# Weight queue, transposes, last pairs, tail squares, output queues and four pads in a one-layer attention kernel

## Chip, core and metric

The kernel runs on one core of one Trainium2 chip, in one launch. The metric is the device time of an execution in microseconds (us). The profile is one execution's trace; its engines are PE (TensorE products, with PEld for their weight loads), DVE (VectorE), ACT (ScalarE), POOL (GpSimd) and SP (SyncE, which issues DMAs).

## What is computed

One decoder layer on x of 256 x 1024 floats, then a final norm:

```
xn   = rmsnorm(x) * norm_g
q,k,v,z = xn @ w_in                  # 1024 x 4096
o    = softmax(q k^T / 8 - slope * distance, causal) v     # 16 heads of 64
h    = x + (o * silu(z)) @ w_out     # 1024 x 1024
out  = rmsnorm(h) * final_g
```

With 256 tokens the block selection of the reference has one block only, so attention is plain causal softmax with a distance bias.

## The kernel before

Every large product is made of three products of rounded parts: each fp32 operand is split into a high part and the rest, and high x high, high x low and low x high are summed in one PSUM bank. So every weight tile must be loaded by DMA, cast on ACT (`split`, L243), and subtracted on DVE (L246) before PE can use it.

The stages follow each other on PE:

- **Start.** 14 products on zeros (`warm`), transposes of x (`x_transpose`, L291, four chunks c of 256 columns, 4 transposes each) and of the gain. x comes in eight DMAs of 128 KB, the value weights in rows of 512 KB (row 0 in two halves), all issued by SP.
- **V** (L313 to 328): for each of 8 rows d of the value weights, four groups of three products with 512 moving columns (the weights move; the gained x, in `gh` and `gl`, is stationary).
- **Z, then Q and K** (`cols_unit`, L272): 8 units for the gate, then 8 pairs of one q unit and one k unit. A unit is 24 products with 256 moving columns (the normed x, in `nh` and `nlo`, moves; the weights, in `wh` and `wl`, are stationary).
- **Pairs** (L443 to 485): after each pair's units, two heads' scores, softmax on DVE and ACT, transposes of the probabilities, product with v, the gate.
- **O** (L497 to 516): output rows like V, for token halves j = 0 and 1; rows 0 to 3 of w_out first, rows 4 to 7 piece by piece (`PIECES`: 512 and 512 columns for j = 0; 512, 256 and 256 for j = 1).
- **Tail** (L507 to 565): for each piece the residual is added on DVE, squares are summed, POOL takes the power -1/2, the result is scaled by it and by final_g and stored.

The order on each engine is not the order in the text. `Plan` (L30) takes every task with an engine, a cost, a due time and its reads and writes, runs a list schedule with these costs (the earliest possible start first, then the smallest due time), and the instructions are emitted in that order. Each engine then executes its own instructions in order. Due times come from constants (`ROW`, `UNIT`, `PAIR`, L176). A due time of `FIRST` (-1000) puts a task ahead of everything that is ready. `load_row` and `load_cols` rotate through five buffers `raw`, `split` through five pairs `wh`, `wl`. All tiles lie one behind the other in SBUF in the order of their `sb` lines (L129 to 152).

Of the kernel before, what the change touches and what calls it, by code (L numbers as in the profile page):

```python
# [106 lines left out]
def hybrid_trunk(ctx: ExitStack, tc: tile.TileContext, x, norm_g, w_in, w_out, final_g, out):  # L107
# [17 lines left out]
    def sb(name, shape, dtype=F32):  # L125
        return one.tile(shape, dtype, name=name)
# [25 lines left out]
    ssf, ssq, rf = sb("ssf", [P, NS, 2]), sb("ssq", [P, 1]), sb("rf", [P, NS])  # L152
    bank = [ps.tile([P, 512], F32, name=f"bank{i}") for i in range(8)]

# [21 lines left out]
    ROW, UNIT = 2.82, 2.81  # L176
    PAIR = 2 * UNIT + 2.3
# [22 lines left out]
    def load_row(key, w, t, c0, due, parts=1):  # L200

        if t % 2 == 0:
            slot[key, t] = next_raw()
        s = slot[key, t] = slot[key, t - t % 2]
        n = D // parts
        for i in range(parts):
            o = (t % 2) * D + i * n
            dma(512 / parts, due, raw[s][:, o:o + n], w[:, t, c0 + i * n:c0 + i * n + n],
                [("raw", s, t % 2, k) for k in range(2)[i if parts == 2 else 0:i + 1 if parts == 2 else 2]])
# [53 lines left out]
    def row_mm(key, t, j, b, cols, ah, al, reads, due, start, stop, first=None):  # L263

        s = spl[key, t]
        n = cols.stop - cols.start
        q = slice(j * P, (j + 1) * P)
        add(T, 0.00137 * n, due,
            lambda: mm3(bank[b][:, :n], ah[:, t, q], al[:, t, q], wh[s][:, cols], wl[s][:, cols], start, stop),
            reads + split_of(s, sorted({cols.start // 512, (cols.stop - 1) // 512})), [("b", b)])  # L270

    def cols_unit(key, u, b, due):  # L272
        s = spl[key, u]
        h_, l_ = (w[s].rearrange("p (t e) -> p t e", t=ND) for w in (wh, wl))

        def step(g):
            for d in (2 * g, 2 * g + 1):
                mm3_cols(bank[b][:, :S], h_[:, d, :], l_[:, d, :], nh[:, d, :], nlo[:, d, :], d == 0, d == ND - 1)
        for g in range(4):
            add(T, 0.70, due + 0.70 * g, lambda g=g: step(g), split_of(s) + [("n", g)], [("b", b)], lat=0.25)  # L280


    add(Q, 0.01, 0.05, lambda: nc.sync.dma_start(gr, norm_g[0].rearrange("(t p) -> t p", p=P)), [], ["gr"])
# [18 lines left out]
    load_row("v", wi, 0, 2 * D, 0.2, parts=2)  # L302
# [140 lines left out]
    for p in range(NP):  # L443
# [9 lines left out]
        E = base + 2 * UNIT + 0.3  # L453
        n, m = p % NQ, p % NN
        add(A, 0.81, base + UNIT + 0.9, lambda p=p, b=bq: hi_q(p, b), [("b", bq)], [("qh", n)])
        add(V, 0.84, base + UNIT + 1.9, lambda p=p, b=bq: lo_q(p, b), [("b", bq), ("qh", n)], [("ql", n)])
        for a in range(2):
            add(A, 0.41, E + 0.4 + 0.4 * a, lambda p=p, b=bk, a=a: hi_k(p, b, a), [("b", bk)], [("kh", n, a)])
            add(Q, 0.2, E + 0.8 + 0.4 * a, lambda p=p, a=a: dup_k(p, a), [("kh", n, a)], [("kd", n, a)])
            add(V, 0.42, E + 1.0 + 0.4 * a, lambda p=p, b=bk, a=a: lo_k(p, b, a), [("b", bk), ("kh", n, a)],  # L460
                [("kl", n, a)])
        add(T, 0.72, FIRST + E, lambda p=p: scores(p),
            [("qh", n), ("ql", n)] + [(w, n, a) for w in ("kh", "kd", "kl") for a in range(2)] + [("kl", n)],
            [("b", 4), ("b", 5)], lat=0.25, slack=0.3)
        for a in range(2):
            h = 2 * p + a
            add(V, 0.87, E + 4.2 + 0.8 * a, lambda p=p, a=a: softmax_max(p, a), [("b", 4 + a), ("bias", h)],
                [("nl", m, a)])
            add(A, 1.28, E + 5.4 + 1.2 * a, lambda p=p, a=a: softmax_exp(p, a), [("nl", m, a)],
                [("e", m, a)] + (["silu"] if p == a == 0 else []))  # L470
        add(V, 1.1, E + 8.4, lambda p=p: softmax_norm(p), [("e", m, 0), ("e", m, 1)], [("pn", m)])
        for a in range(2):
# [3 lines left out]
            add(A, 0.48, E + 10 + 0.5 * a, lambda p=p, a=a, b=b: nc.scalar.copy(pT[p % 2][:, a, :], bank[b][:, :384]),  # L476
# [30 lines left out]
    for j in range(NS):  # L507
# [3 lines left out]
        hg = tail[:, :D]  # L511
        n = len(PIECES[j])
        for t, (b, cols) in enumerate(PIECES[j]):
            for d in range(4, ND):
# [9 lines left out]
            if 0 < t < n - 1:
                add(A, c + 0.2, due + 1, lambda hh=hh, xc=xc: nc.scalar.activation(
                    xc, hh, AF.Square, scale=D ** -0.5, accum_out=ssq), [("hh", j, t)], ["ssq"])
                continue
            if t and n > 2:
                add(V, 0.15, due + 0.9, lambda j=j: nc.vector.tensor_add(ssf[:, j, 0:1], ssf[:, j, 0:1], ssq),
                    ["ssq"], [("ssf", j)])  # L530
            add(V, c + 0.1, due + 1, lambda hh=hh, xc=xc, t=t, j=j: nc.vector.tensor_tensor_reduce(  # L531
                xc, hh, hh, scale=1.0 / D, scalar=ssf[:, j, 0:1] if t else EPS, op0=OP.mult, op1=OP.add,
                accum_out=ssf[:, j, min(t, 1):min(t, 1) + 1]), [("hh", j, t)], [("ssf", j)])
            if t < 1 or j == 0:
                add(V, c, due + 2, lambda hh=hh, cols=cols, hg=hg: nc.vector.tensor_mul(hg[:, cols], hh, fg[:, cols]),
                    [("hh", j, t), "fg"], [("hg", j, t)])
        r = rf[:, j:j + 1]
        add(G, 0.8, due + 1, lambda r=r, j=j: nc.gpsimd.tensor_tensor(r, ssf[:, j, 1:2], mhalf[:, :1], op=OP.pow),
            [("ssf", j)], [("rf", j)])
        rows = slice(j * P, (j + 1) * P)  # L540
        if j == 0:
            add(A, 1.16, due + 3, lambda hg=hg, r=r: nc.scalar.activation(hg, hg, AF.Copy, scale=r),
                [("rf", j), ("hg", j, 0), ("hg", j, 1)], [("y", j)])
            add(Q, 1.5, due + 4, lambda hg=hg, rows=rows: nc.sync.dma_start(out2[rows, :], hg), [("y", j)], ["out0"])
        else:

            add(V, 0.42, due + 2, lambda hg=hg, tail=tail: nc.vector.tensor_mul(
                hg[:, 512:768], tail[:, D + 512:D + 768], fg[:, 512:768]), [("hh", j, 1), "fg"], [("hg", j, 1)])
            add(V, 0.35, due + 3, lambda hg=hg, r=r: nc.vector.tensor_scalar(
                hg[:, 0:256], hg[:, 0:256], r, None, op0=OP.mult), [("rf", j), ("hg", j, 0)], [("y", 0)])  # L550
            add(A, 0.36, due + 3, lambda hg=hg, r=r: nc.scalar.activation(
                hg[:, 256:384], hg[:, 256:384], AF.Copy, scale=r), [("rf", j), ("hg", j, 0)], [("y", 1)])
            add(Q, 0.6, due + 3.5, lambda hg=hg, rows=rows: nc.sync.dma_start(out2[rows, 0:384], hg[:, 0:384]),
                [("y", 0), ("y", 1)], ["out1"])
            add(A, 0.5, due + 3.1, lambda hg=hg, r=r: nc.scalar.activation(
                hg[:, 384:704], hg[:, 384:704], AF.Copy, scale=r), [("rf", j), ("hg", j, 0), ("hg", j, 1)], [("y", 2)])
            add(Q, 0.6, due + 3.6, lambda hg=hg, rows=rows: nc.sync.dma_start(out2[rows, 384:704], hg[:, 384:704]),
                [("y", 2)], ["out2"])
            add(V, 0.48, due + 3.1, lambda hg=hg, tail=tail, r=r: nc.vector.scalar_tensor_tensor(
                hg[:, 768:D], tail[:, D + 768:], r, fg[:, 768:D], op0=OP.mult, op1=OP.mult),  # L560
                [("rf", j), ("hh", j, 2), "fg"], [("y", 3)])
            add(V, 0.25, due + 3.2, lambda hg=hg, r=r: nc.vector.tensor_scalar(
                hg[:, 704:768], hg[:, 704:768], r, None, op0=OP.mult), [("rf", j), ("hg", j, 1)], [("y", 4)])
            add(Q, 0.6, due + 3.7, lambda hg=hg, rows=rows: nc.sync.dma_start(out2[rows, 704:D], hg[:, 704:D]),
                [("y", 3), ("y", 4)], ["out3"])
# [31 lines left out]
```

## Time and profile before

| | |
|---|---|
| median of 3 runs | 155.33 us (154.75 to 155.94) |
| the profiled execution | 153.45 us, span of its instructions 151.7 us |
| busy in the span | PE 141.6, PEld 126.7, DVE 103.5, ACT 97.7, POOL 12.6 us |
| chain that ended last | PE 87%, DVE 3%, issue 2%, DMA 2%, ACT 1%, POOL 1% |
| first product of V, end of the last product of O | 9.04 us, 144.44 us |
| granted clock of TensorE over the run | 0.986 |

Times in the trace are us from the span's start. A timeline row gives the start, the duration, the engine, the line, the operation, the tiles written and read with their shapes, and in brackets how long the engine was idle before and who ended that. A matmul row lasts longer than the distance to the next one, since products overlap in the array; the distance of starts is what a product costs. "SPq" rows are DMA issues.

### The profile page before, as it was taken

Reading aid. Unit: us, or ns where it says so; the run is one execution under the profiler, and the core shown is the slowest. Engines: PE = TensorE matmul, PEld = TensorE weight load, DVE = VectorE, ACT = ScalarE, POOL = GpSimd, SP = SyncE. Lnnn points to the kernel's source line nnn. Section 1 sums busy time; section 2 is a strip of 40 time slices with the busy share of each in tenths; the row PEclk is TensorE's granted clock in tenths of the full one; section 3 lists DMA queues with packets and bytes.
Section 4 is the critical chain, followed back from the end, with each engine's and each line's share of the span. In section 5 each row is a group of like instructions: output and inputs, shape, how many; then the busy total and the mean of one; then the engine's idle time right before and its main releaser. Section 6 shows DMA issues by size and latency. Waiting matters only on the chain.

```text
span 151.7 us, 2722 instructions
## 1 busy us (share of the span) xinstructions
PE 141.6 (93%) x1001; PEld 126.7 (84%) x1001; DVE 103.5 (68%) x220; ACT 97.7 (64%) x212; POOL 12.6 (8%) x21
## 2 busy tenths in 40 slices
PE   6879999999999999999999999999999999999900
PEld 3557887889999999999889898998898888878900
DVE  0468899982633607598599898797895958713970
ACT  8769999760554437269998878588938839510230
POOL 6000100000000000000002011001130402010210
PEclk9999999999999999999999999999999999999995
DMA  3999999999787265619914471260010100000033
GB/s 109 263 302 408 403 368 352 347 349 349 234 260 210 71 180 170 207 35 264 314 49 157 177 257 36 77 242 1 2 35 4 35 0 0 0 0 4 0 138 138
DMA packets 18109, 24.82 MB, mean 164 GB/s; under 512 B 936, under 2 KB 15664, under 8 KB 18096
## 3 DMA queue, kind: packets, MB, share of 16 engines
q1 hardware_dynamic: 18096, 24.65, 49.6%
q8 instruction: 8, 0.13, 0.4%
q14 instruction: 5, 0.04, 0.1%
HBM read 22.55 MB, written 1.05 MB: 156 GB/s over the span
## 4 chain that ended last, share of the span: by engine, by line
PE 87%; DVE 3%; issue 2%; DMA 2%; ACT 1%; POOL 1%; POOLq 0%; SPq 0%; DVEq 0%
PE bank L259 15%; PE bank L260 15%; PE bank L261 15%; PE bank L254 9%; PE bank L256 9%; PE bank L255 9%; PE bank L440 4%; PE bank L433 4%; PE bank L410 3%; PE bank L411 2%; DMA xs<-in_x_dram 2%; PE bank L295 1%; DVE raw L521 1%; DVE xs L531 1%; ACT wh L243 1%
## 5 line engine op out<-in xcount | busy, mean ns | idle before, releaser
L246 DVE TENSOR_TENSOR wl<-raw,wh 128x1024 fp32r<-128x1024 f32 (+1 forms) x41 | 48.7, 1203 | 18.2 <-ACT wh L243 17.7
L259 PE MATMUL bank<-nh,wh 128*128 128x256 f32 x192 | 54.8, 286 | 0.0
L261 PE MATMUL bank<-nh,wl 128*128 128x256 f32 x192 | 53.9, 281 | 0.0
L260 PE MATMUL bank<-nlo,wh 128*128 128x256 f32 x192 | 53.9, 281 | 0.0
L243 ACT CAST wh<-raw 128x1024 fp32r<-128x1024 f32 (+1 forms) x41 | 41.8, 1027 | 2.1 <-DMA raw<-in_w_in_dram 1.1
L259 PEld LDWEIGHTS bank<-nh,wh 128*128 128x128 f32 x192 | 36.2, 189 | 0.6 <-issue 0.5
L260 PEld LDWEIGHTS bank<-nlo,wh 128*128 128x128 f32 x192 | 36.3, 189 | 0.0
L261 PEld LDWEIGHTS bank<-nh,wl 128*128 128x128 f32 x192 | 36.2, 189 | 0.0
L254 PE MATMUL bank<-wh,gh 128*128 128x512 f32 (+1 forms) x72 | 27.4, 381 | 0.0
L256 PE MATMUL bank<-wl,gh 128*128 128x512 f32 (+1 forms) x72 | 26.7, 371 | 0.0
L255 PE MATMUL bank<-wh,gl 128*128 128x512 f32 (+1 forms) x72 | 26.7, 371 | 0.0
L484 POOL TENSOR_TENSOR gl<-gt,gh 128x256 fp32r<-128x256 f32 x8 | 8.1, 1015 | 112.9 <-ACT gh L482 112.9
L256 PEld LDWEIGHTS bank<-wl,gh 128*128 128x128 f32 x72 | 13.6, 188 | 2.8 <-DVE wl L246 0.3
L254 PEld LDWEIGHTS bank<-wh,gh 128*128 128x128 f32 x72 | 13.5, 188 | 2.7 <-issue 0.5
L255 PEld LDWEIGHTS bank<-wh,gl 128*128 128x128 f32 x72 | 13.6, 188 | 2.2
L421 ACT ACTIVATE nl<-nl,st 128x128 f32<-128x128 f32 (+1 forms) x32 | 14.3, 449 | 1.4 <-DVE st L415 1.4
L372 ACT ACTIVATE zs<-bank 128x256 f32<-128x256 f32 x8 | 3.1, 385 | 15.0 <-PE bank L261 15.0
L415 DVE CUSTOM_DVE_ANT_0 nl<-bank,bias 128x128 f32<-128x128 f32 (+1 forms) x32 | 9.5, 353 | 2.8 <-PE bank L411 2.7
L429 DVE TENSOR_TENSOR nl<-nl,st 128x256 f32<-128x256 f32 (+1 forms) x16 | 9.4, 630 | 0.3
L394 ACT CAST kk<-bank 64x256 fp32r<-64x256 f32 x16 | 5.8, 365 | 5.8 <-PE bank L261 5.1
L476 ACT COPY pT<-bank 128x384 f32<-128x384 f32 x16 | 6.9, 482 | 3.6 <-PE bank L433 3.5
L385 ACT ACTIVATE qq<-bank 64x256 fp32r<-64x256 f32 x16 | 6.0, 378 | 3.8 <-PE bank L261 3.5
(68 smaller groups left out, 142.9 us busy)
## 6 DMA issues: line engine op xcount, KB each, us to landing
raw<-in_w_in_dram SPq DMA_DIRECT2D x12, 1024.0 KB, 9.6
raw<-in_w_out_dram SPq DMA_DIRECT2D x8, 512.0 KB, 4.1
raw<-in_w_in_dram SPq DMA_DIRECT2D x7, 512.0 KB, 7.8
xs<-in_x_dram SPq DMA_DIRECT2D x8, 128.0 KB, 2.9
kk<-kk SPq DMA_DIRECT2D x16, 64.0 KB, 1.9
raw<-in_w_in_dram SPq DMA_DIRECT2D x2, 256.0 KB, 3.5
fg<-in_final_g_dram SPq DMA_DIRECT2D x1, 512.0 KB, 13.0
out_dram<-raw SPq DMA_DIRECT2D x1, 512.0 KB, 2.6
```

The lines of the kernel that those rows point to most:

```text
L243: add(A, 0.1 + 0.93 / parts, start - 3.0, lambda hi=hi, sr=sr: nc.scalar.copy(hi, sr), rw, [("wh", s, k) for k in ks])
L246: lambda lo=lo, hi=hi, sr=sr: nc.vector.tensor_sub(lo, sr, hi.bitcast(F32)),
L254: nc.tensor.matmul(acc, ah, bh, start=start, stop=False)
L255: nc.tensor.matmul(acc, al, bh, start=False, stop=False)
L256: nc.tensor.matmul(acc, ah, bl, start=False, stop=stop)
L259: nc.tensor.matmul(acc, ah, bh, start=start, stop=False)
L260: nc.tensor.matmul(acc, ah, bl, start=False, stop=False)
L261: nc.tensor.matmul(acc, al, bh, start=False, stop=stop)
L415: nc.vector.tensor_tensor_reduce(nl[p % NN][:, a, o], bank[4 + a][:, o], bias[:, 2 * p + a, b], scale=1.0, scalar=3.0e38, op0=OP.add, op1= ...
L421: nc.scalar.activation(nl[p % NN][:, a, o], nl[p % NN][:, a, o], AF.Exp, scale=-1.0, bias=st[p % NN][:, 0, a, i:i + 1], accum_out=st[p % N ...
L429: nc.vector.tensor_mul(t, t, r[:, :, i:i + 1].to_broadcast([P, 2, o.stop - o.start]))
L484: lambda p=p: nc.gpsimd.tensor_sub(gl[:, p, :], gt[p % 2], gh[:, p, :].bitcast(F32)),
```

## The change

1. Four unused tiles are put between others: `pad0` (24 floats per partition) ahead of `gh`, `pad1` (16) ahead of `nh`, `pad2` (24) ahead of `wh`, `pad3` (16) ahead of `kk`. Everything behind a pad moves up by 96, 64, 96 and 64 bytes in turn; `raw` moves by 160 bytes, `wh`, `wl` and `qq` by 256, `kk` and later tiles by 320.
2. Row 0 of the value weights is issued by ACT, in two halves, as the first thing in the program; the gain's small DMA is issued first on SP. The planner learns their landing from tasks without instructions.
3. The transposes of x chunks 1 to 3 get due times near the row that needs them, in place of `FIRST`.
4. The due times of pair 6's and pair 7's work on ACT and DVE are 3 and 9 us earlier. Planner costs and constants change.
5. In the tail, squares of the first two pieces of each half go to ACT; DVE joins scale and gain into one operation for j = 0; the three stores of j = 1 are two on SP and one, of 512 columns, on ACT.

```diff
+    sb("pad0", [P, 24])
...
+    sb("pad1", [P, 16])
...
+    sb("pad2", [P, 24])
...
+    sb("pad3", [P, 16])
...
+    for i in range(2):
+        a = slice(i * 512, i * 512 + 512)
+        nc.scalar.dma_start(raw[0][:, a], wi[:, 0, 2 * D + i * 512:2 * D + i * 512 + 512])
+    nc.sync.dma_start(gr, norm_g[0].rearrange("(t p) -> t p", p=P))
...
-    ROW, UNIT = 2.82, 2.81
-    PAIR = 2 * UNIT + 2.3
+    ROW, UNIT = 2.74, 2.73
+    PAIR = 2 * UNIT + 2.5
...
-        add(T, 0.00137 * n, due,
+        add(T, 0.00134 * n, due,
...
-            add(T, 0.70, due + 0.70 * g, lambda g=g: step(g), split_of(s) + [("n", g)], [("b", b)], lat=0.25)
...
+            add(T, 0.683, due + 0.683 * g, lambda g=g: step(g), split_of(s) + [("n", g)], [("b", b)], lat=0.25)
...
+    add("first", 3.4, 0, lambda: None, [], ["gr"])
+    for k in range(2):
+        add("first", 0.9, 1 + k, lambda: None, [], [("raw", 0, 0, k)])
+    slot["v", 0] = next_raw()
...
-    load_row("v", wi, 0, 2 * D, 0.2, parts=2)
...
-        add(T, 0.45, FIRST + c, lambda c=c: x_transpose(c), [("x", c, 0), ("x", c, 1)], [("b", 4 + c % 2)], lat=0.25)
+        add(T, 0.45, FIRST if c == 0 else V0 + 2 * ROW * c - 2.3, lambda c=c: x_transpose(c), [("x", c, 0), ("x", c, 1)], [("b", 4 + c % 2)], lat=0.25)
...
+        L = E - (0, 0, 0, 0, 0, 0, 3, 9)[p]
...
-            add(A, 0.41, E + 0.4 + 0.4 * a, lambda p=p, b=bk, a=a: hi_k(p, b, a), [("b", bk)], [("kh", n, a)])
...
+            add(A, 0.38, L + 0.4 + 0.4 * a, lambda p=p, b=bk, a=a: hi_k(p, b, a), [("b", bk)], [("kh", n, a)])
...
-        add(V, 1.1, E + 8.4, lambda p=p: softmax_norm(p), [("e", m, 0), ("e", m, 1)], [("pn", m)])
+        add(V, 1.6, L + 8.4, lambda p=p: softmax_norm(p), [("e", m, 0), ("e", m, 1)], [("pn", m)])
...
+            add(V, c, due, lambda hh=hh, b=b, w=w, xc=xc: nc.vector.tensor_add(hh, bank[b][:, :w], xc),
+                [("b", b)], [("hh", j, t)] + rw)
+            if t < 2:
+                add(A, c + 0.2, due + 1, lambda hh=hh, xc=xc, j=j, t=t: nc.scalar.activation(
+                    xc, hh, AF.Square, scale=D ** -0.5, accum_out=sq[:, j, t:t + 1]), [("hh", j, t)], [("sq", j, t)])
+            else:
+                add(V, c + 0.1, due + 0.1, lambda hh=hh, xc=xc, j=j: nc.vector.tensor_tensor_reduce(
+                    xc, hh, hh, scale=1.0 / D, scalar=ms[:, j:j + 1], op0=OP.mult, op1=OP.add,
+                    accum_out=sq[:, j, 2:3]), [("hh", j, t), ("ms", j)], [("sq", j, t)])
+            if t == 1:
+                add(V, 0.15, due + 1.5, lambda j=j: nc.vector.scalar_tensor_tensor(
+                    ms[:, j:j + 1], sq[:, j, 0:1], EPS, sq[:, j, 1:2], op0=OP.add, op1=OP.add),
+                    [("sq", j, 0), ("sq", j, 1), "rstd"], [("ms", j)])
...
+            add(G, 0.8, due, lambda r=r: nc.gpsimd.tensor_tensor(r, ms[:, 0:1], mhalf[:, :1], op=OP.pow),
+                [("ms", j)], [("rf", j)])
+            for t in range(2):
+                add(V, 0.75, due + 3 + t, lambda t=t, r=r, hs=hs, ys=ys: nc.vector.scalar_tensor_tensor(
+                    ys[t], hs[t], r, fg[:, t * 512:t * 512 + 512], op0=OP.mult, op1=OP.mult),
+                    [("rf", j), ("hh", j, t), "fg"], [("y", j, t)])
+            add(Q, 1.5, due + 4, lambda tail=tail, rows=rows: nc.sync.dma_start(out2[rows, :], tail[:, :D]),
+                [("y", j, 0), ("y", j, 1)], ["out0"])
+            continue
+        add(G, 0.8, due, lambda r=r: nc.gpsimd.tensor_tensor(r, sq[:, 1, 2:3], mhalf[:, :1], op=OP.pow),
+            [("sq", j, 2)], [("rf", j)])
...
+        for t in range(2):
+            add(V, 0.4 + 0.3 * (1 - t), due + 1 - t, lambda t=t, hs=hs, ys=ys: nc.vector.tensor_mul(
+                ys[t], hs[t], fg[:, PIECES[1][t][1]]),
+                [("hh", j, t), "fg"], [("hg", t)])
+        add(V, 0.48, due + 2, lambda r=r, hs=hs, ys=ys: nc.vector.scalar_tensor_tensor(
+            ys[2], hs[2], r, fg[:, 768:D], op0=OP.mult, op1=OP.mult), [("rf", j), ("hh", j, 2), "fg"], [("y", j, 2)])
+        add(Q, 0.5, due + 3, lambda rows=rows, ys=ys: nc.sync.dma_start(out2[rows, 768:D], ys[2]), [("y", j, 2)],
+            ["out3"])
+        add(V, 0.35, due + 2.1, lambda r=r, ys=ys: nc.vector.tensor_scalar(ys[1], ys[1], r, None, op0=OP.mult),
+            [("rf", j), ("hg", 1)], [("y", j, 1)])
+        add(Q, 0.5, due + 3.1, lambda rows=rows, ys=ys: nc.sync.dma_start(out2[rows, 512:768], ys[1]), [("y", j, 1)],
+            ["out2"])
+        add(A, 0.7, due + 2, lambda r=r, ys=ys: nc.scalar.activation(ys[0], ys[0], AF.Copy, scale=r),
+            [("rf", j), ("hg", 0)], [("y", j, 0)])
+        add(A, 0.45, due + 2.5, lambda rows=rows, ys=ys: nc.scalar.dma_start(out2[rows, 0:512], ys[0]), [("y", j, 0)],
+            ["out1"])
```

## Rows read from the trace of the kernel before

**Rows 1.** Waits of PE, whole span: released by, us in total, times, longest

```profile
PE bank L295 <- DVE gl L322: 1.0, 1, 1.0
PE bank L295 <- DMA xs<-in_x_dram: 0.6, 2, 0.4
```

**Rows 2.** Busy time by stretch: length, engines, PE clock, DMA share, GB/s

```profile
32.50:55.00 22.50, 22.50 (x191) 22.47 (x190) 9.75 (x9) 8.79 (x14) 0.00 (x0) 1.00 0.73 221
...
73.00:82.00 9.00, 8.94 (x75) 8.05 (x74) 8.21 (x21) 8.73 (x23) 1.04 (x1) 1.00 0.40 120
...
118.00:138.80 20.80, 20.80 (x120) 17.01 (x119) 11.78 (x25) 10.07 (x24) 3.18 (x3) 1.00 0.03 7
```

**Rows 3.** Timeline of the start, before 5 us

```profile
0.73 1.28 ACT L157 ACT_TABLE_LOAD   x1 [0.73 <-PEq L583]
0.74 0.86 SPq L194 DMA_DIRECT2D xs<-in_x_dram  x2
1.05 2.10 PE L285 MATMUL bank<-warm 128*128 128x256 bf16 x9 [1.05 <-DVE mhalf L159]
2.93 0.91 SPq L194 DMA_DIRECT2D raw<-in_w_in_dram  x2
...
4.83 0.42 PE L285 MATMUL bank<-warm 128*128 128x256 bf16 x1
```

**Rows 4.** Timeline from the third x chunk to the second row of V

```profile
8.74 0.55 PE L295 MATMUL bank<-ident,xs 128*128 128x128 f32 x3 [0.97 <-DVE gl L322]
9.04 0.48 PE L254 MATMUL bank<-wh,gh 128*128 128x512 f32 x1
10.53 1.05 ACT L243 CAST wh<-raw 128x1024 fp32r<-128x1024 f32 x1 [0.37 <-DMA raw<-in_w_in_dram]
11.22 0.60 PE L295 MATMUL bank<-ident,xs 128*128 128x128 f32 x4
11.61 1.23 DVE L246 TENSOR_TENSOR wl<-raw,wh 128x1024 fp32r<-128x1024 f32 x1 [1.49 <-ACT wh L243]
12.89 0.50 PE L256 MATMUL bank<-wl,gh 128*128 128x512 f32 x1
```

**Rows 5.** Tile raw, 4.9 to 5.2 us: the DMA of weight row 1

```profile
L194 SPq DMA_DIRECT2D raw<-in_w_in_dram x1: 432/432/432, 4.8 to 4.8; - x1
...
DMA to landing us min/median/max: 5.7/5.7/5.7
```

**Rows 6.** Timeline of PE in a Z unit, three products in a row

```profile
37.10 0.28 PE L260 MATMUL bank<-nlo,wh 128*128 128x256 f32 x1
37.23 0.28 PE L261 MATMUL bank<-nh,wl 128*128 128x256 f32 x1
37.34 0.28 PE L259 MATMUL bank<-nh,wh 128*128 128x256 f32 x1
```

**Rows 7.** Timeline of PE in V, two products with two others between them

```profile
24.19 0.40 PE L255 MATMUL bank<-wh,gl 128*128 128x512 f32 x1
...
24.89 0.40 PE L255 MATMUL bank<-wh,gl 128*128 128x512 f32 x1
```

**Rows 8.** Timeline of the tail, from the last product to the last store

```profile
144.16 0.28 PE L256 MATMUL bank<-wl,gh 128*128 128x256 f32 x1
...
144.95 0.42 DVE L521 TENSOR_TENSOR raw<-bank,xs 128x256 f32<-128x256 f32 x1
...
145.35 0.42 DVE L547 TENSOR_TENSOR raw<-raw,fg 128x256 f32<-128x256 f32 x1
145.69 0.48 DVE L531 CUSTOM_DVE_ANT_0 xs<-raw,ssf 128x256 f32<-128x256 f32 x1
...
146.25 0.54 POOL L538 TENSOR_TENSOR rf<-ssf,mhalf 128x1 f32<-128x1 f32 x1 [3.17 <-DVE ssf L531]
146.83 0.48 DVE L559 SCALAR_TENSOR_TENSOR raw<-raw,rf,fg 128x256 f32<-128x256 f32 x1 [0.66 <-POOL rf L538]
...
148.52 0.43 SPq L564 DMA_DIRECT2D out_dram<-raw  x1
```

More of the change, by code (lines that the diff above doesn't have):

```diff
@@ L151, in hybrid_trunk @@
     gt = [sb(f"gt{i}", [P, S]) for i in range(2)]
-    ssf, ssq, rf = sb("ssf", [P, NS, 2]), sb("ssq", [P, 1]), sb("rf", [P, NS])
+    sq, rf = sb("sq", [P, NS, 3]), sb("rf", [P, NS])
     bank = [ps.tile([P, 512], F32, name=f"bank{i}") for i in range(8)]
+    for i in range(2):
+        a = slice(i * 512, i * 512 + 512)
+        nc.scalar.dma_start(raw[0][:, a], wi[:, 0, 2 * D + i * 512:2 * D + i * 512 + 512])
+    nc.sync.dma_start(gr, norm_g[0].rearrange("(t p) -> t p", p=P))
     nc.vector.memset(warm, 0.0)
@@ L200, in load_row @@
     def load_row(key, w, t, c0, due, parts=1):
-        if t % 2 == 0:
+        if t % 2 == 0 and (key, t) not in slot:
             slot[key, t] = next_raw()
@@ L279, in cols_unit @@
         for g in range(4):
-            add(T, 0.70, due + 0.70 * g, lambda g=g: step(g), split_of(s) + [("n", g)], [("b", b)], lat=0.25)
-    add(Q, 0.01, 0.05, lambda: nc.sync.dma_start(gr, norm_g[0].rearrange("(t p) -> t p", p=P)), [], ["gr"])
+            add(T, 0.683, due + 0.683 * g, lambda g=g: step(g), split_of(s) + [("n", g)], [("b", b)], lat=0.25)
[3 more added lines that the diff above has]
+    slot["v", 0] = next_raw()
     for i in range(14):
@@ L309, in hybrid_trunk @@
         load_row("v", wi, t, 2 * D, 0.3 + t)
-    add(T, 0.1, FIRST, g_transpose, ["gr"], [("b", 6)], lat=0.25)
+    add(T, 0.1, FIRST + 1, g_transpose, ["gr"], [("b", 6)], lat=0.25)
     add(V, 0.17, 0, lambda: nc.vector.tensor_copy(gT, bank[6][:, :ND]), [("b", 6)], ["gT"])
     for c in range(4):
-        add(T, 0.45, FIRST + c, lambda c=c: x_transpose(c), [("x", c, 0), ("x", c, 1)], [("b", 4 + c % 2)], lat=0.25)
+        add(T, 0.45, FIRST if c == 0 else V0 + 2 * ROW * c - 2.3, lambda c=c: x_transpose(c), [("x", c, 0), ("x", c, 1)], [("b", 4 + c % 2)], lat=0.25)
         for d in (2 * c, 2 * c + 1):
@@ L457, in hybrid_trunk @@
         for a in range(2):
-            add(A, 0.41, E + 0.4 + 0.4 * a, lambda p=p, b=bk, a=a: hi_k(p, b, a), [("b", bk)], [("kh", n, a)])
-            add(Q, 0.2, E + 0.8 + 0.4 * a, lambda p=p, a=a: dup_k(p, a), [("kh", n, a)], [("kd", n, a)])
-            add(V, 0.42, E + 1.0 + 0.4 * a, lambda p=p, b=bk, a=a: lo_k(p, b, a), [("b", bk), ("kh", n, a)],
+            add(A, 0.38, L + 0.4 + 0.4 * a, lambda p=p, b=bk, a=a: hi_k(p, b, a), [("b", bk)], [("kh", n, a)])
+            add(Q, 0.2, L + 0.8 + 0.4 * a, lambda p=p, a=a: dup_k(p, a), [("kh", n, a)], [("kd", n, a)])
+            add(V, 0.42, L + 1.0 + 0.4 * a, lambda p=p, b=bk, a=a: lo_k(p, b, a), [("b", bk), ("kh", n, a)],
                 [("kl", n, a)])
-        add(T, 0.72, FIRST + E, lambda p=p: scores(p),
+        add(T, 0.97, FIRST + E, lambda p=p: scores(p),
             [("qh", n), ("ql", n)] + [(w, n, a) for w in ("kh", "kd", "kl") for a in range(2)] + [("kl", n)],
@@ L466, in hybrid_trunk @@
             h = 2 * p + a
-            add(V, 0.87, E + 4.2 + 0.8 * a, lambda p=p, a=a: softmax_max(p, a), [("b", 4 + a), ("bias", h)],
+            add(V, 0.58, L + 4.2 + 0.8 * a, lambda p=p, a=a: softmax_max(p, a), [("b", 4 + a), ("bias", h)],
                 [("nl", m, a)])
-            add(A, 1.28, E + 5.4 + 1.2 * a, lambda p=p, a=a: softmax_exp(p, a), [("nl", m, a)],
+            add(A, 1.05, L + 5.4 + 1.2 * a, lambda p=p, a=a: softmax_exp(p, a), [("nl", m, a)],
                 [("e", m, a)] + (["silu"] if p == a == 0 else []))
-        add(V, 1.1, E + 8.4, lambda p=p: softmax_norm(p), [("e", m, 0), ("e", m, 1)], [("pn", m)])
+        add(V, 1.6, L + 8.4, lambda p=p: softmax_norm(p), [("e", m, 0), ("e", m, 1)], [("pn", m)])
         for a in range(2):
@@ L475, in hybrid_trunk @@
                 [("b", b), ("nl", m, a), ("e", m, a)], lat=0.25, slack=0.3)
-            add(A, 0.48, E + 10 + 0.5 * a, lambda p=p, a=a, b=b: nc.scalar.copy(pT[p % 2][:, a, :], bank[b][:, :384]),
+            add(A, 0.45, L + 10 + 0.5 * a, lambda p=p, a=a, b=b: nc.scalar.copy(pT[p % 2][:, a, :], bank[b][:, :384]),
                 [("b", b)], [("pT", p % 2, a)])
@@ L479, in hybrid_trunk @@
             [("pT", p % 2, 0), ("pT", p % 2, 1)] + [("v", j, p // 4) for j in range(NS)], [("b", 7)], lat=0.25, slack=0.3)
-        add(V, 0.43, E + 13, lambda p=p: nc.vector.tensor_mul(gt[p % 2], bank[7][:, :S], zs[:, p, :]),
+        add(V, 0.43, L + 13, lambda p=p: nc.vector.tensor_mul(gt[p % 2], bank[7][:, :S], zs[:, p, :]),
             [("b", 7), ("zs", p)], [("gt", p % 2)])
-        add(A, 0.41, E + 13.6, lambda p=p: nc.scalar.copy(gh[:, p, :], gt[p % 2]), [("gt", p % 2)], [("gh", p)])
+        add(A, 0.41, L + 13.6, lambda p=p: nc.scalar.copy(gh[:, p, :], gt[p % 2]), [("gt", p % 2)], [("gh", p)])
         add(G, 0.75, E + 14.2,
@@ L510, in hybrid_trunk @@
         rw = [("raw", s, i, k) for i in range(2) for k in range(2)]
-        hg = tail[:, :D]
-        n = len(PIECES[j])
+        r = rf[:, j:j + 1]
+        rows = slice(j * P, (j + 1) * P)
+        hs, ys = [], []
         for t, (b, cols) in enumerate(PIECES[j]):
@@ L517, in hybrid_trunk @@
             w = cols.stop - cols.start
-            c = 0.15 + w / 950.0
-            hh = tail[:, D + cols.start:D + cols.stop]
+            c = 0.12 + w / 900.0
+            hh, y = tail[:, D + cols.start:D + cols.stop], tail[:, cols]
+            hs.append(hh)
+            ys.append(y)
             xc = xs[j][:, cols]
-            add(V, c, due + 0.5, lambda hh=hh, b=b, w=w, xc=xc: nc.vector.tensor_add(hh, bank[b][:, :w], xc),
-                [("b", b)], [("hh", j, t)] + (rw if t == 0 else []))
@@ L524, in hybrid_trunk @@
[L524 to L540, printed above, removed]
-        if j == 0:
[L542 to L565, printed above, removed]
```

## The prediction, made before the change was run

> **What bounds the kernel now.** I read the waits of PE first. From the span's start on it waits for other engines only during the start, the last time for the third chunk's transposes [rows 1]; behind the first V product no wait is listed. The busy time by stretch says the same: PE is busy for all of the Z stretch and all of the stretch in which the last pairs and O run [rows 2]. So from 9.04 us [rows 4] to the end of the last product, 144.16 + 0.28 = 144.44 us [rows 8], PE is the bound, at a granted clock of 1.00. Three things can move the time: the spacing of the products, the start, and the 7.3 us from 144.44 to the span's end at 151.7. I looked at each in the timeline.
>
> **Pads.** In the Z stretch 191 products take 22.50 us [rows 2], 0.118 us for 256 columns. The warm-up products at the start, also 256 columns, are spaced (2.10 - 0.42) / 8 = 0.21 us [rows 3], one column a tick at 1.2 GHz; at 2.4 GHz that would be 0.105. So 0.012 to 0.013 us of each product is lost somewhere although neither operand is late, and successive distances jump between 0.13 and 0.11 [rows 6]. The same in V: three products of 512 columns from 24.19 to 24.89 [rows 7], 0.233 each, where 0.21 would be free of loss. The pads change only where the two operands of a product, and what ACT and DVE write beside them, lie relative to each other. No row shows two placements, so the price is bounded: at best the whole loss, 0.012 x 576 (the three lines of the units, 192 each) = 6.9 us and 0.022 x 168 = 3.7 us; at worst every product takes the longest distance seen, which prints as 0.13 [rows 6] and with its rounding is about 0.123, against 0.118: 0.005 x 576 = 2.9 us lost, and in proportion 1 us more for the others. I take a gain of 0.004 per unit product, because single distances of 0.11 stand in the same stream with the same tiles [rows 6], and 0.004 for the others: 0.004 x (576 + 168 + 48 of the 256-column pieces of O) = **3.2 us**; I round to 3.0.
>
> The Trainium skill (TensorE: Matmul & The Clock Gate, step by step) has two independent read ports for the moving operand and the weights, so that a weight load takes nothing from the running product. By that the pads are worth nothing, and the sum below would be 3.0 us smaller. The same page's section on the isolated gap has 2.5 ns over the column time, 109 ns for 256 columns; the 118 ns here disagree with it.
>
> **Start.** The last thing that holds V back is weight row 1, not row 0: issued at 4.82, it lands 5.7 later [rows 3, 5], the cast waits for it until 10.53, the subtraction ends at 12.84, and the product that needs it starts at 12.89 [rows 4]. Removed from SP ahead of row 1 are two DMA issues, 0.91 us [rows 3]; the gain's issue only changes place. Row 0's bytes also start 2.2 us earlier (0.74 against 2.93), beside x. Ends: nothing, if the wire is full and row 1 lands as before, and 0.9 to 1.2 if it keeps its 5.7 us. I take 0.9. Against it: the transposes of chunks 2 and 3 move into the dense stream. Chunk 3 already was there at 11.22 [rows 4]; chunk 2 ran at 8.74 for 0.3 to the first product, in time that was lost anyway, and costs 0.4 now. Chunk 1 fits before row 1's product or costs 0.4 more. Net **0.5 us** gained, from 1.2 gained to 0.8 lost. ACT issues two DMAs, some 0.9 us by SP's rows, ahead of its table load at 0.73 [rows 3]; behind it wait the bias fillings and the first casts. That is hidden as long as ACT catches up by row 1's landing; ACT idles 0.37 just there [rows 4], so at most 0.5 is left if not. x itself starts one issue later on SP, 0.4, and the products of row 0 have more than that to spare since the old first product waited 1.0 for chunk 2 [rows 1].
>
> The skill (DMA: Bandwidth & Descriptors, issuing engines are not separate DMA queues) says that a second issuing engine saves only the issue time. That is the 0.9 above, without the 1.2.
>
> **Last pairs first.** PE has no hole in 118 to 138.8 [rows 2], so nothing is there to gain by itself: 0. It gives the order of the tail: with pair 7 done earlier, O's pieces can finish in the order of their due times, so DVE gets them spread out. The price if it goes wrong: splits of w_out come late behind softmax work, and PE waits. DVE is busy 11.78 of 20.80 us there [rows 2], so there is room. In the densest part of the pairs DVE has 8.21 and ACT 8.73 of 9.00 [rows 2], and PE still lost only 0.06; planner costs are reordered there too. I allow 0 to 0.7 lost.
>
> **Tail.** The chain before: last product ends 144.44; DVE reaches the last add only at 144.95, since it is still on earlier pieces; a multiply of 0.42 (L547) and a small add come between add and square sum (145.69); POOL 146.25; final scale 146.83; last of three stores on one queue issued at 148.52 [rows 8]. After: squares of the large pieces are on ACT, so DVE does less before and the add can start at 144.45 (0.5 gained); the multiply has an earlier due time (144.95 to 145.69 becomes some 0.35: 0.4 gained); behind the scale the two SP stores need its 0.48 us and one more issue of 0.43 instead of three in a row, and ACT's store goes beside them: last issue 0.95 after the scale's start instead of 148.52 - 146.83 = 1.69 (0.7 gained). ACT's own step, a scale of 512 columns, is under the 1.05 us of a 1024-column cast [rows 4], some 0.65 with its overhead, and then an issue of 0.43, so it ends no later than SP's. Its store is 256 KB instead of about 190, which I price at 0.3 more. Sum 1.3; the two new scale operations of j = 0 sit on DVE before the last add and may eat some. I take **1.1 us**, ends 0.3 and 1.6.
>
> **Sum.** 3.0 + 0.5 + 1.1 = 4.6 us. The profiled execution would go from 153.45 (151.7 and 1.75 around it) to 148.8; the median of the runs, 1.88 above it, from 155.33 to **150.7 us**.
>
> **Rivals.**
> *Pads do nothing* (24%). For: the 0.118 may be a fixed cost of fp32r products wherever they lie; nothing in the trace compares placements. Then 0.5 + 1.1 remain: 153.7 us.
> *Pads make it worse* (8%), the slower one: operands that used to miss each other now meet at each product of the units. It decides from 2 ns per product on (1.6 us over 792 products); at the bound of 0.123 it costs 3.9 us, and the time is 155.33 - 1.6 + 3.9 = 157.6 us. Against: no row singles out today's placement as a good one; its distances already reach both 0.11 and 0.13.
> *Pads take most of the loss* (8%): 0.118 to about 0.109, some 7 us with V and O, so 146.7 us. Then DVE and ACT come close to bounding the pairs, and not all would arrive.
> Forecast 60%.
>
> Over 1% (1.55 us, about what a measurement can tell): below 153.8 lies nearly all of the forecast, the third rival and half of the first, 0.79; within 1% the rest of the first and a little of the others, 0.15; slower 0.06. The range takes the forecast's bounds and the first rival: 149.0 to 154.2 us; below lies most of the third rival, above the second and the bad end of the first.
>
> **What would show it.** Spacing in the Z stretch: under 0.116 us per product the pads work, at 0.118 they don't, over 0.12 they harm. Landing of row 1 before 9.8 and its product before 12.2: the start pays; else not. Last store issued under 3 us behind the last product's end instead of 4.1: the tail pays. A wait of PE on L246 or L243 between 20 us and its end would refute that reordering is free. The prediction is wrong if the spacing doesn't change, or if PE gets holes in the pairs or O.

## Result

The kernel after takes **153.46 us** (median; 153.05 to 153.6, 4 runs) against 155.23 (154.75 to 155.94, 4 runs): ratio **0.990 [0.9857, 0.9944]**, which is 1.55 us saved (the medians differ by 1.77). The forecast was 150.7 us, with 4.6 us saved. The sign is right and the time lies in the range, but two thirds of the gain did not come. Repeated later the ratio was 0.9885 [0.9844, 0.9925].

The profiled executions hardly differ: 153.33 (span 151.53) against 153.45 (span 151.67). The profiled execution of before reached TensorE's full clock earlier than its repetition did, as the second experiment shows, so this pair hides most of the gain.

**Profile after.** PE's waits first (released by, total, times, longest):

```profile
PE bank L308 <- DMA xs<-in_x_dram: 3.3, 1, 3.3
PE bank L298 <- DVE mhalf L169: 1.1, 1, 1.1
PE bank L445 <- DVE nl L441: 0.3, 1, 0.3
PE bank L445 <- ACT qq L397: 0.2, 1, 0.2
```

Two things are new against [rows 1]: a wait of 3.3 us for x, and two small holes in the middle. Busy time by stretch (length; PE, PEld, DVE, ACT, POOL; PE clock, DMA share, GB/s) has the holes in the pairs, 0.47 of 9.00 us against 0.06 in [rows 2], and none in the last pairs and O:

```profile
73.00:82.00 9.00, 8.53 (x72) 7.73 (x71) 8.14 (x20) 7.71 (x20) 0.40 (x1) 1.00 0.35 126
114.80:138.80 24.00, 24.00 (x150) 19.85 (x149) 14.23 (x36) 13.22 (x33) 3.62 (x3) 1.00 0.03 7
```

The start, in the timeline:

```profile
0.74 0.87 ACTq L162 DMA_DIRECT2D raw<-in_w_in_dram  x2
...
1.21 3.37 SPq L204 DMA_DIRECT2D xs<-in_x_dram  x6
...
6.49 1.23 PE L308 MATMUL bank<-ident,xs 128*128 128x128 f32 x4 [3.33 <-DMA xs<-in_x_dram]
...
10.21 0.48 PE L264 MATMUL bank<-wh,gh 128*128 128x512 f32 x1
...
12.80 0.39 PE L266 MATMUL bank<-wl,gh 128*128 128x512 f32 x1
...
13.03 0.39 PE L264 MATMUL bank<-wh,gh 128*128 128x512 f32 x1
```

Row 0 leaves first. The two transfers of the first x chunk, issued from 1.21 on, land at 6.35 and 6.78 (before: 3.10 and 4.09), PE can begin on them only at 6.49, and V starts at 10.21 instead of 9.04 [rows 4]. In the repetition (`a0` below) they land at 4.50 and 5.57 and V starts at 9.34. Row 1's first product (13.03) follows row 0's twelve with no wait.

Three products of V (compare [rows 7]) now take 24.64 - 23.96 = 0.68 us instead of 0.70:

```profile
23.96 0.39 PE L266 MATMUL bank<-wl,gh 128*128 128x512 f32 x1
24.19 0.39 PE L264 MATMUL bank<-wh,gh 128*128 128x512 f32 x1
24.42 0.39 PE L265 MATMUL bank<-wh,gl 128*128 128x512 f32 x1
24.64 0.39 PE L266 MATMUL bank<-wl,gh 128*128 128x512 f32 x1
```

The tail, against [rows 8]:

```profile
144.38 0.28 PE L266 MATMUL bank<-wl,gh 128*128 128x256 f32 x1
...
144.51 0.68 DVE L564 TENSOR_TENSOR raw<-raw,fg 128x512 f32<-128x512 f32 x1
145.11 0.42 DVE L537 TENSOR_TENSOR raw<-bank,xs 128x256 f32<-128x256 f32 x1
145.44 0.15 DVE L547 SCALAR_TENSOR_TENSOR ms<-sq 128x1 f32<-128x1 f32 x1
145.51 0.42 DVE L564 TENSOR_TENSOR raw<-raw,fg 128x256 f32<-128x256 f32 x1
145.84 0.48 DVE L543 CUSTOM_DVE_ANT_0 xs<-raw,ms 128x256 f32<-128x256 f32 x1
...
146.41 0.54 POOL L560 TENSOR_TENSOR rf<-sq,mhalf 128x1 f32<-128x1 f32 x1 [5.06 <-DVE sq L543]
146.99 0.72 ACT L575 ACTIVATE raw<-raw,rf 128x512 f32<-128x512 f32 x1 [1.85 <-POOL rf L560]
147.74 0.35 ACTq L577 DMA_DIRECT2D out_dram<-raw  x1
147.89 0.42 SPq L573 DMA_DIRECT2D out_dram<-raw  x1
```

The last add still starts 0.45 us after the last product's end (144.66), since DVE is busy with a multiply, and a second multiply stands ahead of the square. Counted from that end, the scale starts at 2.33 us (before 2.39), the last store is issued at 3.23 (before 4.08), and the span ends at 6.87 (before 7.24).

Sum over this pair: V starts 1.17 us later, the stretch from the first V product to the last product shrinks from 135.40 to 134.44 (-0.96), and the tail by 0.36; together -0.15.

### The profile page after: what moved, and what is told of

It is laid out like the page before. It is cut to its first block, busy times and chain, and to the rows that moved or that the text cites. A ratio compares the mean times of both kernels' runs of the same rounds, so it can differ in the third digit from the quotient of the medians.

```text
span 151.5 us, 2718 instructions
## 1 busy us (share of the span) xinstructions
PE 139.8 (92%) x1001; PEld 126.2 (83%) x1001; DVE 99.8 (66%) x214; ACT 97.9 (65%) x216; POOL 12.6 (8%) x21
## 4 chain that ended last, share of the span: by engine, by line
PE 86%; issue 4%; DMA 3%; DVE 2%; ACT 2%; POOLq 0%; POOL 0%; SPq 0%; DVEq 0%
PE bank L269 15%; PE bank L270 15%; PE bank L271 14%; PE bank L264 9%; PE bank L266 8%; PE bank L265 8%; PE bank L452 4%; PE bank L445 4%; DMA xs<-in_x_dram 3%; PE bank L422 2%; PE bank L423 2%; PE bank L308 2%; ACT xs L540 1%; PE bank L298 1%; DVE nl L441 1%
## 5 line engine op out<-in xcount | busy, mean ns | idle before, releaser
L256 DVE TENSOR_TENSOR wl<-raw,wh 128x1024 fp32r<-128x1024 f32 (+1 forms) x41 | 48.5, 1196 | 18.9 <-ACT wh L253 18.6
L253 ACT CAST wh<-raw 128x1024 fp32r<-128x1024 f32 (+1 forms) x41 | 41.3, 1025 | 3.4 <-DMA raw<-in_w_in_dram 2.8
L413 DVE TENSOR_TENSOR kl<-bank,kk 64x256 fp32r<-64x256 f32 x16 | 6.7, 422 | 4.5 <-ACT kk L406 3.7
```

Of the source, the lines that this page charges most:

```text
L253: add(A, 0.1 + 0.93 / parts, start - 3.0, lambda hi=hi, sr=sr: nc.scalar.copy(hi, sr), rw, [("wh", s, k) for k in ks])
L256: lambda lo=lo, hi=hi, sr=sr: nc.vector.tensor_sub(lo, sr, hi.bitcast(F32)),
```

## Experiments

"Spacing" below is the mean distance between the starts of products that follow each other without a hole; a "unit" product is one of the 256-column products of Z, Q and K. All ratios are to the kernel before, run beside.

### 1. The pads, and what in them acts

`e1_after_no_pads` is the change without its four `sb("pad...")` lines, `e3_before_pads` the kernel before with these four lines alone. The other three put pads into the kernel before:

```diff
 p1:  +pad0 [P, 8]   +pad1 [P, 16]  +pad2 [P, 8]
 p3:  +pad2 [P, 8]
 p5:  +padx [P, 8] ahead of xs, and the four pads of the change
```

> The changed kernel without its four pads. If the pads make the products faster as the two traces suggest (154 products of 512 columns from 233.3 to 229.0 ns, some 550 of 256 columns from 118.3 to 117.5), the spacings go back to 233 and 118.3 and the time rises by about 1.2 us (0.8%) over the changed kernel: 0.998 of before. If the spacing has another cause (the order of work on DVE and ACT), it stays at 229 and 117.5 and the ratio stays at 0.990.

> The kernel before with the four pads alone, planner constants as before. If the pads act on the products: 229 and 117.5 ns, from the first V product to the last end 134.2 us instead of 135.4, ratio 0.992. If they don't: 233 and 118.3 ns, ratio 1.000.

> The kernel before with pads of 8, 16 and 8 floats ahead of gh, nh and wh: gh at 0, nh at 64 and wh at 64 in a partition's bytes modulo 128 (before: 96, 96, 64; after: 64, 0, 64). Theory A (each tensor has to begin at a multiple of 64 bytes): 512-column products 228.5 to 229 ns apart and units in the two spacings 113.3 and 117.8, as with the pads of the change. Theory B (the two tensors of a product must not lie 32 bytes apart modulo 64): the same here. Theory C (what counts is that the stationary and the moving tensor share the place modulo 128): units, now both at 64, nearly all at 113.3, and the 512-column products, now at 0 and 64, 233.4 or in between. Ratio to before 0.985 to 0.996 by A and B, 0.97 to 0.985 by C.

> The kernel before with one pad, of 8 floats, ahead of wh: gh, nh and wh all at 96 modulo 128, so none at a multiple of 64 bytes, but no two 32 apart. Theory A (multiples of 64 bytes): 512-column products 233.3 ns apart and units 118.3 as before, ratio 1.00. Theory B (the distance between the two tensors): 228.5 and 113.3 or 117.8 as with the four pads, ratio 0.985 to 0.996. Neither (only the sum of the bytes in a partition matters): as A.

> The kernel before with the four pads of the change and 8 floats more ahead of the first tensor, so that every tensor stands 32 bytes higher than with the four pads alone and all distances between tensors are kept. Theory D (the distances between a product's tensors decide): 512-column products 228.5 to 229 ns apart, units 113.3 and 117.8, ratio to before 0.985 to 0.996. Theory E (the places themselves decide, such as multiples of 64 bytes): 232.5 to 233.8 and 118 to 120, ratio 0.998 to 1.007.

| kernel | wh from gh, from nh: bytes against before | 512 columns, ns | unit, ns | unit distances of 113 or 114 ns | ratio |
|---|---|---|---|---|---|
| before | 0, 0 | 233.3 | 118.3 | 8 of 549 | 1 |
| e1 | 0, 0 | 233.8 | 118.0 | 14 of 545 | 0.998 [0.9947, 1.0015] |
| p1 | +96, +32 | 233.0 | 119.0 | 3 of 549 | 1.003 [0.9989, 1.0067] |
| p3 | +32, +32 | 232.5 | 119.5 | 3 of 549 | 1.006 [1.0014, 1.011] |
| after | +160, +96 | 229.0 | 117.5 | 39 of 543 | 0.990 [0.9857, 0.9944] |
| e3 | +160, +96 | 228.5 | 116.0 | 197 of 548 | 0.992 [0.9873, 0.9962] |
| p5 | +160, +96, all 32 higher | 228.5 | 116.0 | 215 of 548 | 0.991 [0.9869, 0.9949] |

Pads alone (e3) give the ratio of the whole change; the change without them (e1) is within measurement of nothing. p1 and p3 fell out against every theory that promised them a gain (p1 against A, B and C, p3 against B); p3 is even 0.6% slower than before, beyond its interval, so a pad can cost as well. p5 went against E: a shift of everything by 32 bytes keeps the gain. So, as far as this one shift can show, the distances between the tensors count and not their places. Which of the distances, and why +160 and +96 are good, stays open.

With the four pads the distances of the units are no longer a spread. Before, 342 of 549 lie outside 113, 114 and 117 to 119 ns; after, 7 of 543 (e3 54, p5 5). There are two steady spacings, and whole trains keep one. In e3, 48 to 54 us is such a train of the quick kind; first the timeline, then the busy time by stretch, with 55 products in 6 us (before and after have 53 there; products that reach into the window count):

```profile
49.84 0.28 PE L263 MATMUL bank<-nh,wh 128*128 128x256 f32 x1
49.95 0.28 PE L264 MATMUL bank<-nlo,wh 128*128 128x256 f32 x1
50.06 0.28 PE L265 MATMUL bank<-nh,wl 128*128 128x256 f32 x1
50.18 0.28 PE L263 MATMUL bank<-nh,wh 128*128 128x256 f32 x1
```

```profile
48.00:54.00 6.00, 6.00 (x55) 6.00 (x54) 2.68 (x3) 2.87 (x5) 0.00 (x0) 1.00 0.60 176
```

The forecast's 114 ns is this quick kind; after spends 7% of its units in it, its repetition 16%, e3 and p5 36 to 39%. e3 and p5 run the same instructions in the same order, and in both the longest quick train is one of 167 distances, from 47.6 to 66.4 us and from 45.8 to 64.6. f1h and g2h below have the same pads in a changed kernel and also reach 39 and 36%, with units at 116.0 and 116.2 ns. So the same pads bring 0.8 to 2.3 ns per unit product. What starts and ends a quick train was not tested.

### 2. The start

`b0` is the kernel before, unchanged. `e2` is the change with the start of before (row 0 on SP, transposes at `FIRST`). The next three, in short:

```diff
 g1:  ScalarE's two row-0 DMAs behind `nc.scalar.activation(tabl, ...)`
 f1h: planner's numbers of before; row 0 on SP again; transposes as in the change
 g2h: planner's numbers of before; row 0 on ScalarE behind make_bias(0); gr behind x chunk 0
```

> The kernel before, unchanged. Theory S (the start costs, pads and tail pay, and the one profiled execution of before is typical): first V product near 9.0 us, 233 ns per 512-column product, 118.3 ns per unit product, the last product at 144.4, span near 151.7. Rival R (that profiled execution was an early one and ordinary ones start later): first V product at 10 us or later, with the spacings unchanged, span 152.5 to 154. The ratio to before is 1.000 for both and shows what the comparison can tell.

> The changed kernel with the start of before: row 0 and the gain issued by SP in the planned order, x transposes at the front. Theory S: x lands near 4.1 us again instead of 6.8, PE no longer waits 3.3 us for it, the first V product comes near 9.0 instead of 10.2, the time falls by 0.8 to 1.2 us below the changed kernel, ratio 0.983. Rival R: the new start was no loss in ordinary executions; no difference or a rise of up to 1 us, ratio 0.990 to 0.996.

> The kernel after, with ScalarE issuing row 0's two transfers behind its table load and first activation (about 3.1 us instead of 0.74). Theory (row 0 on a second queue takes the engines away from the x chunks): the two transfers of x chunk 0 land at 3.2 to 4.6 us as in the kernel before, not at 6.35 and 6.78, row 0 lands at 6 to 7.5, the first V product starts at 8.3 to 9.3 instead of 10.1 to 10.2, and the time is 0.5 to 1.5 us under the kernel after's 153.5: ratio to before 0.980 to 0.988. Rival (x is late for another reason, or row 0 now becomes the last to arrive): first V product at 10 or later, ratio 0.988 to 0.998 as for the kernel after.

> The kernel after with the planner's numbers of before, and row 0 back on SP's queue behind x chunks 0 and 1 (the x transposes stay behind the first products). Theory S (ScalarE's queue takes the engines from the x chunks, and only the later transposes are worth something): x chunk 0 lands at 3.1 and 3.6 to 4.3 us, the first V product starts at 8.0 to 8.6, row 1 still lands at 10.3 to 11, the 3 products a row wait for it once; end of TensorE's work 0 to 0.8 us earlier than with ScalarE's queue, ratio to before 0.976 to 0.986. Rival R (the earlier issue of row 1 is what counts, as the prediction said): a wait of 1 us or more before row 1's products, and a ratio 0.004 to 0.008 above the kernel's with ScalarE's queue, 0.990 to 0.996.

> The kernel after with the planner's numbers of before, row 0 on ScalarE's queue but issued only behind the first bias activation (about 2.2 to 3.5 us instead of 0.74), and x chunk 0 ahead of the gains on SP. Theory S: x chunk 0 lands by 4.3 us, row 0 by 6.5 to 7.3, row 1 by 9.0 to 10, first V product 8.3 to 9.0 and no wait for row 1; ratio to before 0.974 to 0.983, the lowest of all. Rival R (only the sum of bytes counts: x chunks 0 and 1, row 0 and row 1 come over the same engines whatever their order): first V product 9.1 to 10.2, ratio 0.982 to 0.990 as with the planner's numbers undone alone.

b0: 1.0026 [0.9983, 1.007], yet its profiled execution differs from the one that the prediction read. Its first V product comes at 9.49 and the next ones 0.43 apart (timeline):

```profile
9.49 0.78 PE L254 MATMUL bank<-wh,gh 128*128 128x512 f32 x1
10.06 0.63 PE L255 MATMUL bank<-wh,gl 128*128 128x512 f32 x1
10.49 0.63 PE L256 MATMUL bank<-wl,gh 128*128 128x512 f32 x1
```

0.43 us for 512 columns (512 / 0.43 = 1.19 columns per ns) is the 1.2 GHz level. From 12.0 on they are 0.233 apart. The busy time by stretch shows a clock of 1.00 for b0's slow stretch too, and the mean clock is 0.986 in both profiles of the kernel before, so neither number gives it away; in p1's trace, with the same spacing, it shows the step (busy time by stretch):

```profile
7.80:14.40 6.60, 5.33 (x17) 4.36 (x17) 4.85 (x12) 5.00 (x9) 0.00 (x0) 0.50 0.98 359
14.60:16.60 2.00, 2.00 (x10) 1.60 (x9) 1.47 (x3) 2.00 (x5) 0.71 (x1) 1.00 1.03 422
```

By the clock records of the traces, the full clock that lasts to the end of the products begins at 7.5 us in the profile of before that the prediction read, ahead of its first V product, and at 12.0 in b0, 13.2 in e3, 14.5 in p1, 9.8 in after, 12.0 in its repetition, 9.0 to 11.9 in h1, g1 and f1h. (p1 had the full clock from 4.3 us on and lost it at 7.7, after PE had idled from 5.80 to 7.49 for x.) In three of the 18 profiles it begins ahead of the first V product: before, after and h1. So the prediction read a lucky execution: b0's last product ends 1.18 us later (145.62 against 144.44) with the same instructions, and against b0 the kernel after is 1.33 us shorter in span (152.86 to 151.53), near the timed difference.

e2: 0.9945 [0.9883, 1.0007], 0.0045 above after, unresolved. f1h: 0.9866 [0.9806, 0.9927], x chunk 0 at 3.13 and 3.96, first V product at 8.96, row 1 landing at 10.34. h1 (below), which differs from it by row 0 on ScalarE's queue and the place of the gain's DMA, has 0.9865. So x does come earlier without that queue, as theory S says, but the time is the same. In its profile f1h's V products run 0.43 apart until 11.9, while h1 has the full clock from 9.0. The pair differs in more than the start, though: f1h's order has the transposes of the fourth x chunk at 13.2 instead of 23.8 us, and its units are 1.2 ns closer, which is 0.7 us over 576 products. g1 tells nothing on its question, since its issue moved by 0.3 us only. It stands behind the activation in the program, and goes out before it (timeline of ScalarE):

```profile
0.73 1.28 ACT L164 ACT_TABLE_LOAD   x1 [0.73 <-PEq L596]
1.04 0.86 ACTq L167 DMA_DIRECT2D raw<-in_w_in_dram  x2
2.03 0.20 ACT L164 ACTIVATE tabl<-warm 128x1 f32<-128x1 bf16 x1
```

(0.9895 [0.9859, 0.9931], as after.) g2h: 1.0101 [1.0055, 1.0147], against both theories. Its row 0 was issued at 5.33, later than planned, behind all eight x transfers and two weight rows; PE waited 2.1 us for its cast, and V began at 12.67.

### 3. The planner's numbers

`h1_planner_undone`: the change with `ROW`, `UNIT`, `PAIR`, the costs of the attention and the due times of the last two pairs as before. `a0` is the kernel after, unchanged.

```diff
-    ROW, UNIT = 2.74, 2.73
+    ROW, UNIT = 2.82, 2.81
...
-        L = E - (0, 0, 0, 0, 0, 0, 3, 9)[p]
+        L = E
```

> The kernel after with the planner's numbers of before (row, unit and pair lengths, the attention's costs, no earlier due times for the last two pairs). Theory (the new numbers cost the 0.5 to 0.6 us of holes that TensorE has at 73 to 75 us in every kernel that has them): no holes between the units there, and a time 0.4 to 0.8 us under the kernel after's: ratio to before 0.982 to 0.988. Rival (the new numbers are paid back in the attention or at the end): the holes go, but the end of TensorE's work or the tail grows by as much; ratio 0.988 to 0.995.

> The kernel after, unchanged, so that it stands on one chip beside the next two. If the verdict of the first comparison holds: ratio to before 0.985 to 0.994. The first x chunk lands at 4.8 to 6.8 us and the first V product starts at 9.1 to 10.3, by how fast the chip's first transfers move; 512-column products 228.5 to 229 ns apart.

h1: 0.9865 [0.9812, 0.9918]; a0: 0.9885 [0.9844, 0.9925], in another session. The holes go (h1 has 0.07 us of them from 12 us on; after 0.47, a0 0.51), and the stretch from PE's end to the span's end grows from 6.87 to 7.17. So by these traces 0.30 of the 0.40 us is paid back at the end, as the rival says; the rest is under what these runs resolve.

### 4. The tail

`t1` moves ScalarE's store to SP, `t2` leaves it out (512 columns of the last row block are not written). `t3` is the kernel after, `t3h` is h1, each with this line, which puts both multiplies behind the sum of squares:

```diff
-                [("hh", j, t), "fg"], [("hg", t)])
+                [("hh", j, t), "fg", ("sq", j, 2)], [("hg", t)])
```

> The kernel after with the 256 KB store of ScalarE's queue on SP's instead. Theory W (two queues at once share the wire, so the second one bought little): the last store is issued 0.3 to 0.5 us later, lands 1.9 to 2.3 us after its issue, and the stretch from TensorE's end to the span's end is 6.85 to 7.1 us, within 0.2 of the kernel after. Rival Q (the second queue is worth its issue): 7.2 us or more.

> The kernel after with ScalarE's store of 256 KB left out (so 512 columns of the last row block are not written). Theory W (sharing makes the last SP store land late): it lands 2.0 to 2.15 us after its issue as in the kernel before, and the stretch shrinks to 6.3 to 6.5 us. Rival (the store takes 2.5 us by itself): 2.5 to 2.6 and 6.8 to 6.9.

> The kernel after with the two multiplications by the final gains of the last row block behind the sum of squares on DVE, not ahead of the last addition and of the squares. Theory D (DVE's order holds the last addition): the last addition starts within 0.05 us of TensorE's end instead of 0.46, the square 0.6 us earlier, the ScalarE scale 0.35 to 0.45 us earlier (then held by the moved multiplication), and the stretch from TensorE's end to the end of the span is 6.45 to 6.6 us instead of 6.88. Rival W (the wire and the landing set the end): the stretch stays at 6.8 to 6.9. Ratio to before 0.983 to 0.990 by D, 0.986 to 0.993 by W.

> The same reordering under the planner's numbers of before. By D the stretch from TensorE's end to the end of the span falls from 7.17 to 6.6 to 6.85 us and the ratio to before is 0.979 to 0.988, the lowest so far with no holes at 73 to 75 us; by W the stretch stays at 7.1 to 7.2 and the ratio at 0.983 to 0.992.

From PE's end to the span's end: after 6.87, t1 **6.94**, t2 **6.19**, t3 **6.57**; h1 7.17, t3h **6.87**. t1 and t2 are one execution each, but the stretch repeats well: in after, a0, g1 and e1, whose tails are the same, it is 6.85 to 6.88. The second queue is worth 0.07 us. Without it the last issue comes 0.48 us later (t1: 149.29 - 145.58 = 3.71 after PE's end), but from the last issue to the span's end it is 3.23 us in t1 and 3.64 in after (151.53 - 147.89); with ScalarE's store left out it is 2.95 (t2: 151.48 - 148.53). That is theory W, with a larger effect in t2 than it gave. Theory D holds too: t3's 6.57 lies in its 6.45 to 6.6, t3h's 6.87 just over its 6.85. DVE in t3 (last product's end 144.85):

```profile
144.37 0.94 DVE L537 TENSOR_TENSOR raw<-bank,xs 128x256 f32<-128x256 f32 x2
145.36 0.16 DVE L547 SCALAR_TENSOR_TENSOR ms<-sq 128x1 f32<-128x1 f32 x1
145.56 0.48 DVE L543 CUSTOM_DVE_ANT_0 xs<-raw,ms 128x256 f32<-128x256 f32 x1
...
145.97 1.02 DVE L564 TENSOR_TENSOR raw<-raw,fg 128x256 f32<-128x256 f32 x2
```

The second add starts at once and the square 0.71 us after PE's end instead of 1.18; the small sum (L547) ahead of it waits for ScalarE's squares. The multiplies then hold ScalarE's scale (147.08, so 2.23 after PE's end against 2.33, where D said 0.35 to 0.45 less), and the last issue comes at 2.99 instead of 3.23. Timed: t3 **0.9841** [0.9783, 0.9898], 152.77 us; t3h 0.9851 [0.9809, 0.9894], 152.64 us. These are the lowest of all; the step below the kernel after is in the traces, the timed intervals overlap.

## Why the prediction was wrong

Of the 4.6 us that were forecast, 3.0 were for the pads and 1.6 for the start and the tail. Timed alone, the pads gave 1.3 us (e3) and the rest of the change 0.3 (e1, whose interval reaches from 0.8 gained to 0.2 lost). That the measured time lies next to the first rival's 153.7 us is chance: that rival gives the pads nothing.

- **Pads: right mechanism, wrong size; this is the step that failed most.** "I take a gain of 0.004 per unit product" was the term. In the kernel after, the 576 unit products gave 0.0008 (118.27 to 117.45 ns, 0.5 us), and 0.0023 in e3. In the Z stretch of the kernel after, from 36 to 55 us, not one distance is of the quick kind and the mean is 117.7 ns; by the prediction's own sign the pads would do nothing there. The single distances of 0.11 in [rows 6] were taken for what the pads would make common. They are part of a spread; the quick train exists, but most units do not run in it. The 512-column products gave 0.0043 as forecast (233.3 to 229.0 ns; 168 of them, 0.7 us), but no row showed a shorter distance among them, so that hit was luck. Together this is 1.2 us in after and 2.1 in e3, of which 1.3 were timed. By the two read ports of the Trainium skill (TensorE: Matmul & The Clock Gate, step by step) the pads would give nothing; the ratios of e3 (0.992) and p5 (0.991) speak against that.
- **Start: 0.5 us gained was forecast.** "The products of row 0 have more than that to spare" failed. Behind row 0's bytes, x chunk 0 came not 0.4 but 2.7 to 3.3 us later (6.35 and 6.78 instead of 3.10 and 4.09; 1.4 to 1.5 later in the repetition), and row 1's product came at 13.03 instead of under 12.2. With row 0 back on SP, in f1h, x lands at 3.13 and 3.96 again. Why the late x cost less time than the profile suggests is argued and not shown: in 15 of the 18 profiles at least the first V product runs at 1.2 GHz, so a V that starts earlier spends more products at 0.43 us each. What the start is worth is not resolved (e2 0.0045 above after; f1h and h1 0.0001 apart, with units of different spacing).
- **Tail: 1.1 us forecast, 0.36 measured.** The last issue did come under the 4.1 us, at 3.23, though not under the 3 that was to show it. Of the 0.9 for an earlier add and an earlier multiply 0.06 came, because the order on DVE kept a multiply ahead of the add and one ahead of the square (t3 gets 0.3 more out of that order). The 0.7 at the issue came (0.79), but from the last issue to the span's end it took 0.49 longer (3.64 against 3.15); I had priced the larger store at 0.3. The Trainium skill (DMA: Bandwidth & Descriptors, issuing engines are not separate DMA queues) has it that a second issuing engine saves only issue time. The trace agrees that it is no more: of 0.48 us of issue, t1 loses 0.07 at the end.
- **Last pairs and planner: 0, with 0.7 lost allowed for.** The order was not free: there are 0.47 us of holes at 73 to 75 us, with the waits on ScalarE's `qq` and DVE's `nl`, not on the casts and subtractions (L243 and L246 before, L253 and L256 after), and by h1 0.30 of that came back in the tail.
- **The sum's base.** The prediction took one profiled execution that lay 1.88 us below the median and carried the difference over unexplained. Against b0's profile 1.18 of it is the start of V and the clock of that execution; the rest stays open.

## What to carry over

Read how long a resource is lost as a distribution, not from its best single rows: a quick distance among slow ones does not say that a change will hold it. Profile the kernel before twice when the argument rests on its first microseconds, and read the clock there from the spacing of products. Ahead of a tail's critical operation look at the order on its engine: work that can wait for an idle stretch (here the multiplies, while POOL works) is worth moving before queues are: by these traces 0.30 us against 0.07.

## What was not expected

- In this kernel the spacing of fp32r products depends on how far apart the tensors lie in SBUF: 512 columns take 233 or 228.5 ns, 256 columns 118 to 119.5 or one of two steady values, 113.3 and 117.8.
- The full TensorE clock that lasts begins at 7.5 (before) to 14.9 us (e2) in executions of much the same start, whose PE begins at 1 us; in g2h, where PE waits 2.1 us until 12.67, at 18.0.
- In g1 a DMA that stands behind an activation in ScalarE's program was issued 1.0 us ahead of that activation's execution (1.04 against 2.03).
